# Another rate of gathers in each stage of a gMLP, SSD and PEER block

## The chip, the core and the metric

The kernel runs on one core of a Trainium2 chip. The metric is device time in microseconds (us) of one execution, as the median of several runs. Lower is better.

## The reference

One transformer block over 1024 tokens of width 1024, in float32. Cut to what matters here:

```python
h = x @ w_in                       # -> uv, z, xbc, dt_raw, gate_pre
ya = gmlp_branch(uv, ...) @ gm_w_out
yb = ssd_branch(z, xbc, dt_raw, ...) @ ssd_w_out
merged = gates[0] * ya + gates[1] * yb
x1 = layer_norm(ALPHA * x + merged @ w_o)
q = x1 @ w_q                       # 8 heads, two halves, 128 keys each
...                                # top 16 of each half, top 16 of their sums: 128 experts a token
act = gelu(einsum('tkd,td->tk', u_tab[experts], x1))
ch = einsum('tk,tkd->td', softmax_gates * act, v_tab[experts])
ple = sigmoid(x1 @ ple_w_gate + b) * (p @ ple_w_proj)
out = layer_norm(ALPHA * x1 + ch + ple)
```

`u_tab` and `v_tab` have 16384 rows of 1024 floats each, so each token needs 128 rows of either table.

## The kernel before

**Groups and stages.** The 1024 tokens are worked through in three groups of 2, 3 and 3 blocks of 128 tokens (`GROUPS`, here groups 0, 1 and 2). `front(gi)` (L218) runs one group through its stages: gMLP, SSD, merge, query (the product with `w_o`, the normalization, the products with `w_q`, the top 16, the PLE gate). Every matrix product is made of three fp32r passes (`mm3`, L155 to L157), and every weight tile is read by SyncE's DMA queue (`raw`), cast on ScalarE (`whi`, L149) and its rest taken on VectorE (`wlo`, L150).

**Two ways to apply the experts.** For groups 0 and 1 the rows that each token needs are gathered (`gather`, L835): one indirect DMA on GpSimd's queue brings 128 rows of 4 KB, one for each token of a block, into one of `RING` = 12 buffers named `row`. A U row is multiplied with the token and summed on VectorE (L856). Four V rows at a time go through products on TensorE (`pacc`, L898). A block takes 128 U and 128 V gathers, five blocks 1280 in all. For group 2 nothing is gathered: its stage "gates" (`dense_gates`, with `dense_scores` beside it) writes the gates of all 16384 experts to DRAM, and its stage "dense" (L988) multiplies the tokens with both whole tables, in 16 steps of 8 tiles of experts. The scores of 48 of the 128 tiles are computed ahead and kept in DRAM (`s`); the step that comes before one of these blocks of tiles reads them back (`ew<-s`, L1014), the others compute them.

**Side by side.** The gathers of group 0 are written into the program beside the stages of group 1, those of group 1 beside the rest of it and beside group 2. Their order within a gather group is: 70 U rows, then U and V rows in turn, and at the end 64 V rows alone. The order is written out by hand: `front` is a generator that yields a cost after each piece of work; the loop at the end of `block_kernel` (L1064 to L1074) adds the cost times the stage's rate to what is owed, and writes gathers, at 1.47 each, until nothing is owed. Which rate counts is `SIDE[phase[0]]` (L46):

```python
for cost in front(gi):
    owed += cost * SIDE[phase[0]]
    if not gate_t:
        owed = 0.0
    while side and owed > 0:
        step = next(side[0], None)
        ...
        owed -= step
```

The costs are in units of `UNIT` × blocks / 4, which is 4.01 for three blocks. A group of three blocks yields 33.6 units in the gMLP stage (8 for `w_v`, 9.6 for `w_u`, 16 for gates and output); in group 1 the last 24.4 of them come after the first gates exist. The SSD stage yields 66.2, the merge 16, the query stage 36.6 in a gather group and 58.6 in the dense group (with 22 score tiles), the gates 219.5 in plain cost, the dense stage 208 units and 14.4. What is left when `front(2)` has ended is written after it. `phase[0]` is 0 in the gMLP stage, 1 from the SSD stage to the end of the merge, 2 in the query stage, 3 in the gates and 4 in the dense stage.

**Other order.** A planner orders the instructions of each engine after the order written, with weights moved ahead by fixed offsets. A U row's multiply stands at least 6 gathers (`LAG`) behind its gather, and the products of four V rows at least 4 (`QLAG`). When the last gather block has 16 gathers left, two further ring buffers are filled with `ln2_g` and `ln2_b` (`finish_loads`, L793) for its normalization (`finish`, L799); the last dense step does the same for its own.

Of the kernel before, what the change touches and what calls it, by code (L numbers as in the profile page):

```python
# [42 lines left out]
AHEAD_G = 40  # L43
LEAD = 50
UNIT = 5.35
SIDE = (0.82, 0.78, 0.80, 0.66, 0.78)  # L46
ALPHA = 2 ** 0.25
EPS = 1e-5

# [32 lines left out]
def block_kernel(ctx, tc, a, out):  # L82
# [114 lines left out]
    ps, ps_es, phase, tk_, selects = {}, [None], [0], [None], []  # L197
# [20 lines left out]
    def front(gi):  # L218
# [310 lines left out]
            V.reciprocal(rrow, rrow)  # L529


        mp_es = ExitStack()
        mp = mp_es.enter_context(tc.tile_pool(name="mp", bufs=1, side=other))
        mh = mp.tile([128, 8, T], F32R, name="mh")
# [528 lines left out]
    for gi in range(NG):  # L1063
# [7 lines that stand above are left out]
                if step is None:  # L1071
                    side.pop(0)
                else:
                    owed -= step  # L1074
        if GROUPS[gi][1] == "gather":
            selects += [select(gi, c) for c in range(GROUPS[gi][0])]
            side += [experts([(gi, c, r0 + c * 128) for c in range(GROUPS[gi][0])])]
        r0 += GROUPS[gi][0] * 128
# [79 lines left out]
```

## Time and profile before

| | |
|---|---|
| median of 3 runs | 3757.99 us (3755.95 to 3758.19) |
| profiled execution, its own time | 3754.28 us |
| its span, first to last instruction | 3752.6 us |
| busy share of the span | TensorE 92%, VectorE 78%, ScalarE 47%, GpSimd 42% |
| granted TensorE clock, mean | 0.962 |
| moved by DMA | 1183.88 MB, 315 GB/s on average |

The stages in the span, read from the first and last instruction of their tiles (us from its start):

| stage | group 0 | group 1 | group 2 |
|---|---|---|---|
| gMLP | 0 to 112 | 520 to 713 (gathers from 563) | 1345 to 1548 |
| SSD | 112 to 340 | 713 to 1060 | 1548 to 1905 |
| merge | 340 to 400 | 1060 to 1137 | 1905 to 2002 |
| query | 400 to 520 | 1137 to 1345 | 2002 to 2310 |
| gates | | | 2310 to 2625 |
| dense | | | 2625 to 3673 |
| rest | | | 3673 to 3752.6 |

In the profile PE is TensorE's products, PEld its weight loads, DVE VectorE, ACT ScalarE, POOL GpSimd, SP SyncE. A busy share says how full an engine was in a stretch; PEclk is the granted share of TensorE's full clock, and the DMA share is the mean of the core's 16 DMA engines.

### The profile page before, as it was taken

How to read it: one execution, taken by the hardware profiler on the slowest of the kernel's cores; microseconds unless marked ns; L12 is line 12 of the kernel's file. 1: busy time of each engine (PE TensorE's matmuls, PEld its weight loads, DVE VectorE, ACT ScalarE, POOL GpSimd, SP SyncE). 2: the span in 40 equal slices, each digit the busy share in tenths (PEclk: the TensorE clock that was granted, in tenths of full speed). 3: DMA queues.
4: the chain of work that ended last, by engine and by line, in shares of the span. 5: the costliest groups of instructions: out<-in, count | busy, mean ns of one | idle time of the engine just before them, and what ended most of it. 6: DMA issues, size and time to landing. Idle time of an engine off the chain costs nothing. (4 is left out here: it accounts for less than half of the span.)

```text
span 3752.6 us, 59429 instructions
## 1 busy us (share of the span) xinstructions
PE 3439.9 (92%) x21390; PEld 2939.4 (78%) x21390; DVE 2935.7 (78%) x6823; ACT 1754.2 (47%) x2671; POOL 1569.2 (42%) x1310
## 2 busy tenths in 40 slices
PE   9899996999998988999987989889989999999995
PEld 8888896888887977888777878777768878778771
DVE  6677898898987989894698999997676676676652
ACT  6888443475752333475742334675333323233220
POOL 0000004744455444543455455334455455455544
PEclk9999998999999999999999999999999999999997
DMA  6444647989899787989899899899999999999987
GB/s 212 160 164 160 229 174 249 389 308 356 311 369 391 288 305 285 358 308 323 295 326 337 302 337 371 329 335 370 349 378 379 363 360 370 357 365 395 367 313 283
DMA packets 405703, 1183.88 MB, mean 315 GB/s; under 512 B 40736, under 2 KB 135968, under 8 KB 402336
## 3 DMA queue, kind: packets, MB, share of 16 engines
q0 software_dynamic: 187488, 682.71, 48.5%
q1 hardware_dynamic: 217200, 494.76, 36.8%
q8 instruction: 168, 2.75, 0.3%
q10 hardware_dynamic: 720, 2.62, 0.2%
q14 instruction: 127, 1.04, 0.1%
HBM read 1121.01 MB, written 58.92 MB: 314 GB/s over the span
## 5 line engine op out<-in xcount | busy, mean ns | idle before, releaser
L149 ACT CAST whi<-raw 128x1024 fp32r<-128x1024 f32 (+1 forms) x676 | 700.5, 1041 | 1127.2 <-PE mm L156 582.2
L837 POOL DMA_INDIRECT row<-in_peer_u_dram,idx x640 | 796.3, 1244 | 1004.3 <-PE pacc L898 376.2
L157 PE MATMUL mm<-xh,wlo 128*128 128x384 f32 (+2 forms) x3160 | 1055.3, 335 | 57.4 <-DVE wlo L150 50.5
L150 DVE TENSOR_TENSOR wlo<-raw,whi 128x1024 fp32r<-128x1024 f32 (+1 forms) x676 | 817.1, 1211 | 371.0 <-ACT whi L149 298.7
L155 PE MATMUL mm<-xh,whi 128*128 128x384 f32 (+2 forms) x3160 | 1060.6, 336 | 38.0 <-ACT whi L149 27.2
L156 PE MATMUL mm<-xl,whi 128*128 128x384 f32 (+2 forms) x3160 | 1046.8, 331 | 0.6 <-DVE xl L139 0.6
L837 POOL DMA_INDIRECT row<-in_peer_v_dram,idxT x640 | 758.9, 1186 | 681.9 <-DVE row L856 210.9
L856 DVE SCALAR_TENSOR_TENSOR row<-row,x1b 128x1024 f32<-128x1024 f32 x640 | 773.6, 1217 | 22.9 <-DMA row<-in_peer_u_dram,idx 18.5
L155 PEld LDWEIGHTS mm<-xh,whi 128*128 128x128 f32 (+1 forms) x3160 | 606.9, 192 | 93.4 <-ACT whi L149 51.5
L157 PEld LDWEIGHTS mm<-xh,wlo 128*128 128x128 f32 (+1 forms) x3160 | 606.1, 192 | 78.1 <-DVE wlo L150 60.1
L156 PEld LDWEIGHTS mm<-xl,whi 128*128 128x128 f32 (+1 forms) x3160 | 606.3, 192 | 9.5 <-issue 2.8
L898 PE MATMUL pacc<-row,zw 128*32 128x512 f32 x2560 | 321.3, 621 | 39.2 <-DMA row<-in_peer_v_dram,idxT 39.1
L155 PE MATMUL po<-whi,ewh 128*128 128x512 f32 x768 | 313.9, 409 | 20.1 <-DVE eacc L1051 17.9
L156 PE MATMUL po<-wlo,ewh 128*128 128x512 f32 x768 | 309.4, 403 | 17.1 <-DVE wlo L150 17.0
L157 PE MATMUL po<-whi,ewl 128*128 128x512 f32 x768 | 308.2, 401 | 0.0
L898 PEld LDWEIGHTS pacc<-row,zw 128*32 128x32 f32 x2560 | 68.5, 111 | 193.9 <-issue 140.6
L155 PEld LDWEIGHTS po<-whi,ewh 128*128 128x128 f32 x768 | 147.3, 192 | 86.3 <-DVE eacc L1051 19.9
L156 PEld LDWEIGHTS po<-wlo,ewh 128*128 128x128 f32 x768 | 147.5, 192 | 50.4 <-DVE wlo L150 18.5
L852 POOL DMA_DIRECT2D x1b<-x x5 | 3.0, 606 | 434.2 <-DMA x<-x 434.1
L138 ACT CAST ewh<-ew 128x384 fp32r<-128x384 f32 x128 | 65.6, 513 | 242.4 <-DVE ew L1019 175.3
L157 PEld LDWEIGHTS po<-whi,ewl 128*128 128x128 f32 x768 | 147.4, 192 | 36.1
L981 PE MATMUL mt<-o,o 128*128 128x128 f32 x768 | 148.9, 302 | 15.1 <-DVE o L979 6.0
(275 smaller groups left out, 5609.3 us busy)
## 6 DMA issues: line engine op xcount, KB each, us to landing
raw<-in_peer_uT_dram SPq DMA_DIRECT2D x128, 512.0 KB
raw<-in_peer_vd_dram SPq DMA_DIRECT2D x128, 512.0 KB
raw<-in_w_xbc_dram SPq DMA_DIRECT2D x96, 512.0 KB
raw<-in_w_g_dram SPq DMA_DIRECT2D x48, 512.0 KB
raw<-in_w_z_dram SPq DMA_DIRECT2D x48, 512.0 KB
raw<-in_ssd_w_out_dram SPq DMA_DIRECT2D x48, 512.0 KB
raw<-in_w_q_dram SPq DMA_DIRECT2D x48, 512.0 KB
g<-gt SPq DMA_DIRECT2D x24, 1024.0 KB
```

The source lines that it names most:

```text
L138: A.copy(hi, src)
L149: A.copy(hi, raw)
L150: V.tensor_sub(lo, raw, hi.bitcast(F32))
L155: PE.matmul(p, lhsT=lh, rhs=rh, start=start, stop=False, skip_group_check=skip)
L156: PE.matmul(p, lhsT=lh, rhs=rl, start=False, stop=False, skip_group_check=skip)
L157: PE.matmul(p, lhsT=ll, rhs=rh, start=False, stop=stop, skip_group_check=skip)
L837: g = POOL.indirect_dma_start(out=t, out_offset=None, in_=a[tab], in_offset=bass.IndirectOffsetOnAxis(ap=ix, axis=0))
L852: POOL.dma_start(x1, x1_d[gi, c])
L856: u = V.scalar_tensor_tensor(t, t, 1.0, x1, op0=OP.mult, op1=OP.mult, accum_out=act[:, k:k + 1])
L898: return PE.matmul(pacc[q * 32:q * 32 + 32, h * 512:h * 512 + 512], lhsT=zws[z][:, q, r % 4, :], rhs=ts[q][:, h * 512:h * 512 + 512], star ...
L981: PE.matmul(p[:, i, :], lhsT=o1, rhs=o2, start=True, stop=True)
```

## The change

`SIDE` gets new rates and a sixth entry, and the merge gets a phase of its own. The gMLP stage goes from 0.82 to 0.70, SSD from 0.78 to 0.82, the query stage from 0.80 to 0.68, the dense stage from 0.78 to 0.86, and the merge from the 0.78 of the SSD stage to 1.1. The gates keep 0.66.

```diff
-SIDE = (0.82, 0.78, 0.80, 0.66, 0.78)
+SIDE = (0.70, 0.82, 0.68, 0.66, 0.86, 1.1)
...
             V.reciprocal(rrow, rrow)


+        phase[0] = 5
         mp_es = ExitStack()
         mp = mp_es.enter_context(tc.tile_pool(name="mp", bufs=1, side=other))
```

## Rows read from the trace of the kernel before

**Rows 1.** The page: TensorE's busy time, and GpSimd's DMA queue (packets, MB, share).

```profile
PE 3439.9 (92%) x21390; PEld 2939.4 (78%) x21390; DVE 2935.7 (78%) x6823; ACT 1754.2 (47%) x2671; POOL 1569.2 (42%) x1310
...
q0 software_dynamic: 187488, 682.71, 48.5%
```

**Rows 2.** Windows by stage: length, PE, PEld, DVE, ACT, POOL, clock, DMA share, GB/s.

```profile
563.00:713.00 150.00, 120.25 (x640) 114.69 (x641) 140.34 (x315) 51.41 (x68) 90.59 (x65) 0.90 0.83 307
713.00:1060.00 347.00, 335.55 (x2199) 296.87 (x2198) 306.47 (x610) 239.74 (x386) 169.91 (x140) 0.99 0.89 331
1060.00:1137.00 77.00, 72.76 (x442) 64.54 (x441) 65.58 (x108) 27.48 (x35) 43.98 (x36) 0.98 0.98 374
1137.00:1195.00 58.00, 52.55 (x424) 44.49 (x423) 46.60 (x81) 20.11 (x32) 32.45 (x28) 0.98 1.02 395
1195.00:1297.00 102.00, 96.25 (x590) 84.98 (x591) 92.03 (x415) 31.52 (x49) 43.48 (x36) 0.96 0.84 316
...
1345.00:1460.00 115.00, 97.07 (x620) 80.95 (x620) 103.77 (x348) 51.89 (x73) 56.87 (x45) 0.92 0.84 309
...
1905.00:2002.00 97.00, 79.61 (x430) 74.49 (x428) 94.88 (x157) 34.11 (x48) 53.98 (x43) 0.93 0.95 346
...
2075.00:2165.00 90.00, 88.53 (x553) 78.35 (x552) 89.75 (x413) 30.46 (x48) 37.51 (x34) 1.00 0.85 302
2165.00:2310.00 145.00, 131.97 (x840) 117.56 (x839) 137.78 (x453) 55.03 (x64) 74.89 (x61) 0.96 0.94 355
...
2625.00:3673.00 1048.00, 1005.72 (x5131) 794.35 (x5133) 693.61 (x1067) 319.63 (x427) 529.60 (x447) 0.98 0.97 362
3673.00:3752.60 79.60, 34.76 (x193) 6.47 (x192) 15.25 (x29) 5.63 (x7) 38.83 (x40) 0.68 0.77 291
```

**Rows 3.** Windows view of the gathers alone (L837): POOL busy and count, then as above.

```profile
1060.00:1137.00 77.00, 43.98 (x36) 0.98 0.98 374
...
2625.00:3673.00 1048.00, 524.42 (x438) 0.98 0.97 362
3673.00:3752.60 79.60, 37.68 (x38) 0.68 0.77 291
```

**Rows 4.** Windows view of dense steps, all engines: two long, short, long, last.

```profile
2832.40:2907.60 75.20, 75.20 (x401) 61.85 (x400) 52.01 (x77) 23.10 (x30) 45.91 (x36) 1.00 0.99 379
2907.60:2984.90 77.30, 77.30 (x418) 62.17 (x416) 50.64 (x75) 25.43 (x34) 34.09 (x33) 1.00 0.97 358
2984.90:3033.00 48.10, 42.07 (x181) 30.35 (x178) 32.22 (x52) 11.68 (x17) 22.55 (x20) 0.89 0.99 357
...
3355.30:3430.60 75.30, 75.30 (x401) 61.85 (x400) 55.14 (x84) 25.54 (x32) 46.03 (x39) 1.00 1.03 403
...
3632.90:3673.00 40.10, 40.10 (x200) 28.10 (x200) 14.39 (x23) 7.34 (x8) 15.56 (x16) 1.00 0.74 260
```

**Rows 5.** Waits (total, times, longest), in dense and in 622 to 712.

```profile
DVE ew L1019 <- DMA ew<-s: 66.0, 16, 10.2
...
PEld mm L157 <- DVE wlo L150: 16.7, 3, 14.5
```

**Rows 6.** The chain that ended last, its end: start, us, what.

```profile
3731.78 6.26 DMA row<-in_peer_v_dram,idxT
3738.09 2.98 PE pacc L898 x16
...
3747.16 1.22 DVE x1b L808
```

**Rows 7.** Groups of instructions: the U multiply and its sum's read (count, busy, mean ns).

```profile
L856 DVE SCALAR_TENSOR_TENSOR row<-row,x1b 128x1024 f32<-128x1024 f32 x640 | 773.6, 1217 | 22.9 <-DMA row<-in_peer_u_dram,idx 18.5 <-issue 3.4
...
L856 DVE DVE_READ_ACCUMULATOR row<-row,x1b 128x1 f32 x640 | 51.7, 81 | 0.0
```

**Rows 8.** Windows view of the U multiplies alone (L856): DVE busy and count, then as above.

```profile
563.00:713.00 150.00, 68.46 (x115) 0.90 0.83 307
...
1905.00:2002.00 97.00, 50.36 (x84) 0.93 0.95 346
```

## The prediction

> **What bounds the kernel now.** I first read the page. TensorE is busy 92% of the span and GpSimd's DMA queue alone takes 48.5% of the 16 DMA engines [rows 1]. An average over unlike stages decides nothing, so I cut the span into stages with the windows view [rows 2]. In group 1's and group 2's gMLP and query stages VectorE is the fullest engine: 0.94 of 563:713, 0.90 of 1345:1460, 0.90 of 1195:1297, 1.00 of 2075:2165, 0.95 of 2165:2310, while the DMA share there is 0.83 to 0.94. The SSD stage (713:1060) has TensorE at 0.97 and DMA at 0.89. Merge and dense have DMA at 0.95 to 0.98. So the change takes gathers out of stages that are full on VectorE and puts them where DMA is full.
>
> A view of gathers per stage says whether the hand-made pacing is what the chip runs. The code gives a stage its cost × rate / 1.47 gathers. The merge of group 1 costs 16 units of 4.01 = 64.2, × 0.78 / 1.47 = 34, and the trace has 36; dense costs 208 units of 4.01 + 14 = 849, so 450, and the trace has 438; the last stretch gets the rest of 1280, 42, and the trace has 38 [rows 3]. The order written is the order run, within a ring buffer's run-ahead.
>
> Then the dense steps one by one [rows 4]. A step has 144 products with the expert table. In long steps (nine of sixteen) eight score tiles are computed as well, and TensorE is busy all of it: 75.2 us with 401 TensorE instructions, 77.3 with 418. The difference, one more group of 16 for four V rows, is 2.1 us. Short steps (five) take scores back from DRAM: 48.1 us, TensorE at 0.93 of full clock or under, DMA at 0.99. The last step does the same products in 40.1. In the view of waits, the multiply by the gates waits 66.0 us for these scores [rows 5]. Short steps are DMA-bound; long ones are bound by TensorE with DMA just below its limit. Last, the chain that ended last: after the products end at 3673, 38 gathers, a last landing (6.26 us), the product (2.98) and a normalization fill 79.6 us [rows 2, 3, 6].
>
> **Prices of a gather.** DMA: the queue's 48.5% of 3752.6 us over 1302 transfers of 512 KB (1280 gathers and 22 plain loads) is 1.40 us each [rows 1]. VectorE: a U row costs 1217 + 81 ns = 1.30 us [rows 7], a V row almost nothing; where they alternate, 0.65. TensorE: a V row costs 2.1 / 4 = 0.52 [rows 4], on average 0.26.
>
> **The change, part by part.** By the same formula:
> - gMLP, 0.82 to 0.70: group 1 has 24.4 units left once gates exist, so 55 to 47 gathers; group 2, 33.6 units, 75 to 64.
> - SSD, 0.78 to 0.82: 66 units, 141 to 148 in each group.
> - merge, 0.78 to 1.1: 34 to 48 in each.
> - query, 0.80 to 0.68: group 1, 36.6 units, 80 to 68; group 2, 58.6 units, 128 to 109.
> - gates, unchanged: 98.
> - dense, 0.78 to 0.86: 450 to 497.
> - rest, after everything: 42 to 4.
>
> No instruction is added or removed, and no wait is written in; all costs come from where the rows stand in in-order queues.
>
> *Rest.* 38 gathers were issued in the 59 us from 3673 to 3731.8 [rows 3, 6]. With 4 left, what remains is the dense blocks' own normalization and one landing, product and finish, as in the chain from 3731.78 on (about 21 us), plus a few gathers: some 30 us instead of 79.6. Gain 50; bounds 45 (a few more left over) and 59 (none).
>
> *Dense, +46.* Five short steps get 2 more each; they are DMA-bound, so 2 × 1.40 each, +14. Nine long steps get 3.6 more each. By TensorE that is 3.6 × 0.26 = 0.9 us a step; by DMA 5.0, less the about 2% (1.6 us) that DMA was free. One step moved 403 GB/s at a share of 1.03 and took no longer than the others [rows 4], so part of it still fits: I take 2 a step, +18. The other steps: +3. Sum +35; bounds 46 × 0.26 = 12 and 46 × 1.40 = 65. Here also the last gather block's two ln2 loads now fall into the last dense step, where the dense group holds two of the ring's 12 buffers as well; eight are left for the gathers. The last step's DMA share is 0.74 [rows 4], which covers this; without that cover it is a landing, 6 us, inside the bound.
>
> *Merge, +14 in each.* In group 1 DMA is full from 1060 to 1195 (0.98, 1.02) [rows 2]: 14 × 1.40 = 20, less what was taken from the query products right behind (3 gathers, 4 us) and what the next stage, at 0.84, can take over through prefetch: +10, bounds 4 (TensorE) and 20. In group 2 the merge lies in the stretch where group 1's U rows come alone: 50.4 us of U work in 97, VectorE at 0.98 [rows 2, 8]. The rows now land before the merge's own multiplies and weight splits in VectorE's queue, and TensorE waits for these: 14 × 1.30 = 18, less 3 in the stage behind, +15; bounds 9 and 20. Together +25.
>
> The merge's DMA row in group 1 is 0.98 at 374 GB/s, though half the requests come from GpSimd and half from SyncE. The Trainium skill (DMA: Bandwidth & Descriptors, section Issuing engines are not separate DMA queues) says that transfers of all issuing engines end on the same 16 DMA engines and interleave. By that rule every added gather delays weights, in merge and dense alike: the slower rival below. The sum above does not use it.
>
> *SSD, +7 in each.* TensorE: 7 × 0.26 = 2 each. Group 1 also gets U rows that left the gMLP stage (8 × 1.30) on a VectorE at 0.88: hidden behind TensorE, 1 more. +5; bounds 0 and 15.
>
> *gMLP, −8 and −11.* Group 1's are all U rows: 8 × 1.30 = 10 us less VectorE in a stage where it is 0.94 full. But the longest wait of TensorE there is one of 14.5 us for one weight split [rows 5], which a burst of VectorE work causes and a lower rate does not remove: −6. Group 2: 11 × 0.65 = 7, so −6. Together −12; bounds 0 and −18.
>
> *Query, −12 and −19.* × 0.65: 8 and 12 us of VectorE; TensorE is busy all but 2% of 2075:2165 [rows 2], so there only part is given back: −7 and −11; bounds 0 and −30, the latter at DMA price where its share is over 0.94.
>
> **Sum:** −50 + 35 + 25 + 5 − 12 − 18 = −15 us, from the profiled 3754.3 to 3739. The median is 3.7 above the profiled execution, so 3743.
>
> **Rivals.**
> 1. *DMA is the price everywhere (slower).* Dense pays 65 and merge 40: −50 + 65 + 40 + 5 − 12 − 18 = +30, 3788. For it: shares of 0.97 and 0.98 [rows 2]. Against it: TensorE without a gap in all long steps [rows 4]. It decides once a gather in dense costs over about 1.1 us (50 / 46), the merge as above.
> 2. *DMA has room (much faster).* Dense pays TensorE's price, 12, merge 4 + 15 (VectorE stays full there): −50 + 12 + 19 + 5 − 30 = −44, 3714. For it: the step at 403 GB/s. Against it: short steps wait for DMA. The Trainium skill (Perfetto Trace Analysis, section Identifying the Most-Contended Engine) says that occupancy of the DMA engines misleads and HBM use should be read instead. By that rule dense, at 362 GB/s on average [rows 2], still has 403 − 362 = 41 GB/s, a tenth, and this rival would hold; the short steps at 357 and waiting speak against it here.
> 3. *The relieved stages do not get shorter,* since bursts (top-16, selection) and not the gathers make VectorE late: −50 + 35 + 25 + 5 = +15, 3773. For it: the 14.5 us wait. Against it: U work alone is 68 of 150 us there.
> 4. *The pacing is not followed:* no change, 3758. Against it: [rows 3].
>
> **How the numbers follow.** What a measurement of this kernel can tell from no change is about 0.2%, 7.5 us. My forecast, with its own range of −38 to +5: 0.49; rival 1: 0.18; rival 2: 0.15; rival 3: 0.15; rival 4: 0.03. Faster: 0.15 and four fifths of mine, 0.54. Within 0.2%: a fifth of mine, a third of rival 3, rival 4: 0.18. Slower: rival 1 and the rest of rival 3: 0.28. The range goes from rival 2 (−44, a little more if the query stages return the full price) to rival 1 (+30): 3706 to 3788.
>
> **What would show it.** Right: some 4 gathers after the last dense product and a stretch there of about 30 us; long dense steps of 77 to 79 us and short ones of 50 to 51; both merges at 85 to 115 us; gMLP stages each some 6 us shorter. Wrong: long steps over 80 us or merges 20 us longer (rival 1), long steps at 76 (rival 2), gMLP and query lengths unchanged (rival 3). The prediction fails most easily in the price of a gather in a long dense step, which decides 30 of its us.

## The result and the profile after

The changed kernel takes 3731.78 us (median of 5 runs, 3727.95 to 3742.35) against 3757.99 us: ratio 0.9936, interval 0.9919 to 0.9952, so 0.6% faster. Its profiled execution took 3731.47 us with a span of 3729.8. On a second chip, where the kernel before had a median of 3772.24, the ratio was 0.993 (0.991 to 0.9949).

The first fence has the windows view of the changed kernel by stage, with the columns of [rows 2]; the borders are moved with the stages.

```profile
564.00:709.00 145.00, 119.73 (x632) 115.00 (x632) 135.00 (x305) 50.73 (x67) 81.93 (x59) 0.91 0.82 303
709.00:1064.00 355.00, 341.01 (x2241) 297.57 (x2241) 312.69 (x622) 237.89 (x384) 182.50 (x146) 0.99 0.90 328
1064.00:1150.00 86.00, 75.69 (x435) 64.54 (x434) 70.78 (x120) 26.68 (x35) 54.01 (x45) 0.94 1.02 398
...
1909.00:2024.00 115.00, 85.61 (x439) 79.73 (x436) 112.16 (x186) 34.12 (x48) 77.20 (x59) 0.87 0.98 365
...
2084.00:2174.00 90.00, 88.65 (x554) 80.08 (x553) 87.62 (x400) 29.93 (x48) 39.05 (x33) 1.00 0.78 288
2174.00:2309.00 135.00, 125.31 (x794) 112.41 (x794) 131.00 (x444) 52.04 (x62) 60.22 (x49) 0.97 0.93 339
...
2622.00:3709.30 1087.30, 1034.78 (x5321) 801.74 (x5319) 700.47 (x1079) 318.78 (x427) 562.46 (x495) 0.97 0.99 370
3709.30:3729.80 20.50, 3.82 (x33) 0.81 (x32) 14.21 (x25) 5.62 (x7) 0.56 (x1) 0.75 0.44 171
```

Against [rows 2], dense is some 39 us longer with DMA at 0.99, the stretch behind it fell from 79.6 to 20.5 us, and group 2's merge (1909:2024) has VectorE at 0.98 and TensorE at 0.74. The same view for the gathers alone, as in [rows 3]:

```profile
2622.00:3709.30 1087.30, 556.16 (x484) 0.97 0.99 370
3709.30:3729.80 20.50, 0.56 (x1) 0.75 0.44 171
```

One gather is issued behind dense instead of 38. The chain that ended last shows what is left there (columns as in [rows 6]): dense's own last sum and normalization (`eacc`) and then the gather block's (`x1b`), on VectorE with ScalarE between, and no row's landing any more.

```profile
3709.39 0.68 DVE eacc L1052
...
3714.64 2.35 DVE eacc L1058 x2
3717.06 1.12 DVE x1b L803
...
3724.73 1.23 DVE x1b L809
```

The dense steps, as in [rows 4]: the first, a long one, two short ones, the last long one and the last.

```profile
2661.30:2706.60 45.30, 41.97 (x194) 29.20 (x194) 30.85 (x49) 12.98 (x18) 19.94 (x17) 0.96 1.04 375
...
2837.30:2914.60 77.30, 77.30 (x418) 62.25 (x417) 53.59 (x81) 23.09 (x30) 41.94 (x38) 1.00 1.01 392
...
2991.80:3042.80 51.00, 41.45 (x182) 29.37 (x179) 33.14 (x60) 11.73 (x17) 19.78 (x21) 0.90 0.99 362
3317.50:3372.10 54.60, 41.22 (x181) 29.80 (x178) 36.07 (x58) 11.26 (x16) 28.45 (x26) 0.84 1.04 383
...
3579.70:3667.20 87.50, 87.50 (x498) 63.85 (x496) 33.21 (x46) 24.52 (x32) 35.03 (x37) 1.00 0.88 322
3667.20:3709.30 42.10, 42.10 (x216) 28.41 (x212) 13.79 (x19) 7.33 (x8) 19.39 (x21) 1.00 0.78 272
```

TensorE still has no gap in a long step, though DMA is now at 1.01 there; 77.3 instead of 75.2 us is one more group of four V rows. The last long step is 87.5 us, all of it TensorE: V rows that used to run behind dense are now in it. Before, this step and the first were:

```profile
2664.10:2701.90 37.80, 37.80 (x178) 27.78 (x177) 29.46 (x49) 13.26 (x18) 20.05 (x17) 1.00 1.03 374
...
3553.50:3632.90 79.40, 79.40 (x435) 62.63 (x433) 45.91 (x71) 24.79 (x33) 41.34 (x35) 1.00 0.90 342
```

The first step also reads eight scores back, so six steps are short, not five.

### The profile page after: what moved, and what is told of

It is laid out like the page before. It is cut to its first block, busy times and chain, and to the rows that moved or that the text cites. A ratio compares the mean times of both kernels' runs of the same rounds, so it can differ in the third digit from the quotient of the medians.

```text
span 3729.8 us, 59409 instructions
## 1 busy us (share of the span) xinstructions
PE 3437.4 (92%) x21390; PEld 2944.0 (79%) x21390; DVE 2934.5 (79%) x6823; ACT 1744.7 (47%) x2666; POOL 1551.4 (42%) x1310
## 5 line engine op out<-in xcount | busy, mean ns | idle before, releaser
L838 POOL DMA_INDIRECT row<-in_peer_u_dram,idx x640 | 786.8, 1229 | 937.6 <-PE pacc L899 299.3
L157 PE MATMUL mm<-xh,wlo 128*128 128x384 f32 (+2 forms) x3160 | 1054.9, 334 | 42.7 <-DVE wlo L150 41.0
L838 POOL DMA_INDIRECT row<-in_peer_v_dram,idxT x640 | 750.7, 1173 | 746.0 <-DVE row L857 245.0
L899 PE MATMUL pacc<-row,zw 128*32 128x512 f32 x2560 | 312.0, 605 | 15.1 <-DMA row<-in_peer_v_dram,idxT 15.1
L899 PEld LDWEIGHTS pacc<-row,zw 128*32 128x32 f32 x2560 | 67.2, 109 | 155.7 <-issue 131.5
L155 PE MATMUL mm<-whi,xh 128*128 128x256 f32 x512 | 148.4, 290 | 11.9 <-ACT whi L149 10.4
```

Source lines behind the costliest of these rows:

```text
L155: PE.matmul(p, lhsT=lh, rhs=rh, start=start, stop=False, skip_group_check=skip)
L157: PE.matmul(p, lhsT=ll, rhs=rh, start=False, stop=stop, skip_group_check=skip)
L838: g = POOL.indirect_dma_start(out=t, out_offset=None, in_=a[tab], in_offset=bass.IndirectOffsetOnAxis(ap=ix, axis=0))
L899: return PE.matmul(pacc[q * 32:q * 32 + 32, h * 512:h * 512 + 512], lhsT=zws[z][:, q, r % 4, :], rhs=ts[q][:, h * 512:h * 512 + 512], star ...
```

## The stages of all runs

A stage is counted here from its first instruction of one fixed kind (such as the merge's first sigmoid) to that of the next stage, so that runs can be compared; "relief" means the lower rates of the gMLP and query stages. Lengths in us, one profiled execution each. The first two columns are from one chip; the others were run where the kernel before had medians of 3772 to 3773 us, the last two beside the third and fourth.

| stage | before | after | before, 2nd | after, 2nd | dense only | merge only | relief only | more in SSD | merge back | dense 0.90 |
|---|---|---|---|---|---|---|---|---|---|---|
| gMLP 1 | 153.4 | 148.2 | 158.3 | 148.1 | 154.6 | 155.7 | 148.8 | 148.3 | 147.9 | 149.1 |
| SSD 1 | 348.3 | 356.7 | 352.3 | 362.3 | 350.6 | 352.2 | 348.3 | 370.4 | 358.1 | 357.5 |
| merge 1 | 83.1 | 92.1 | 82.6 | 91.3 | 83.7 | 92.3 | 82.7 | 90.9 | 84.1 | 84.9 |
| query 1 | 191.3 | 185.7 | 196.3 | 182.2 | 196.9 | 199.1 | 178.3 | 184.9 | 183.4 | 180.9 |
| gMLP 2 | 212.6 | 208.5 | 212.6 | 210.5 | 211.7 | 212.6 | 208.8 | 201.9 | 210.2 | 207.8 |
| SSD 2 | 372.7 | 373.5 | 375.3 | 372.8 | 378.5 | 389.4 | 357.9 | 406.1 | 362.6 | 362.0 |
| merge 2 | 89.2 | 107.2 | 87.0 | 107.8 | 89.9 | 106.1 | 94.0 | 98.9 | 94.5 | 96.6 |
| query 2 | 320.5 | 297.3 | 323.5 | 298.1 | 323.0 | 302.3 | 323.3 | 299.4 | 317.8 | 315.7 |
| gates | 329.3 | 327.4 | 338.5 | 333.6 | 334.3 | 329.7 | 339.3 | 335.6 | 336.7 | 333.4 |
| dense | 1008.9 | 1048.1 | 1008.9 | 1054.9 | 1048.5 | 1031.0 | 1016.5 | 1044.3 | 1040.7 | 1073.7 |
| rest | 79.6 | 20.4 | 80.5 | 20.4 | 19.4 | 42.3 | 147.4 | 19.9 | 58.3 | 30.4 |
| ratio to before, same chip | | 0.9936 | | 0.9930 | 0.9945 | 1.0024 | 1.0114 | 0.9976 | 0.9955 | 0.9971 |

## The experiments

Theory A is that of the prediction: a gather costs in each stage what the engine that is full there asks for it. Its rivals: only what is left at the end counts (B); the relief of the stages full on VectorE is the gain (C).

**One part at a time.** All of these are the changed kernel with other rates. Dense alone:

```diff
-SIDE = (0.70, 0.82, 0.68, 0.66, 0.86, 1.1)
+SIDE = (0.82, 0.78, 0.80, 0.66, 0.86, 0.78)
```

> The rates of before everywhere, only dense at 0.86: 42 gathers move from the stretch after the dense products into dense, none is left. Theory A (each stage has its own price, set by the engine that is full there): dense pays 0.85 us a gather as in the changed kernel, 36 us longer, the stretch at the end 59 us shorter, in all 20 to 25 us faster than before, within 5 us of the whole change. Theory B (only what is left at the end counts, a gather costs the same in every other stage): 20 to 25 us faster as well. Theory C (the relief of the stages full on VectorE is the gain): no gain, within 7 us of before.

Ratio 0.9945 (0.9928 to 0.9962), 21 us of 3773: A and B both give this, C falls. The dense stage is 1048.5 us and the rest 19.4, as in the whole change. So dense alone brings nearly all of the gain; what the other rates add, 3 to 6 us, is within the intervals.

The merge alone:

```diff
+SIDE = (0.82, 0.78, 0.80, 0.66, 0.78, 1.1)
```

> The rates of before everywhere, only the merge at 1.1: 14 more gathers in each merge, 14 instead of 42 left at the end. Theory A: group 1's merge 9 us longer, group 2's 18 us longer, of which the query stage behind gives some 10 back, the end 28 x 1.5 = 42 us shorter: 20 to 30 us faster. Theory B: 42 us less at the end and 28 x 0.85 = 24 more before it, 18 us faster, with both merges equally longer (12 us each). Theory C: slower or the same, since both merges are full and nothing is relieved.

Ratio 1.0024 (1.0008 to 1.004): 9 us slower, where A and B expected 18 to 30 us faster and only C "slower or the same". Against the first profile both merges are longer by what A said (9 and 17 us) and the rest is 37 us shorter. But two stages with unchanged rates are longer too, SSD 2 by 17 us and dense by 22. A had counted rows and not which rows: when more are taken early, group 1's lone U rows begin 14 places earlier, in SSD 2, and lone V rows of the end come into dense. The windows of the U multiplies in SSD 2 and of the V products in dense, in this run:

```profile
1577.40:1966.90 389.50, 59.36 (x98) 0.96 0.85 301
```

```profile
2704.90:3736.00 1031.10, 115.64 (x968) 25.14 (x968) 0.97 0.97 357
```

The same stretches of the kernel before:

```profile
1552.40:1925.10 372.70, 50.99 (x84) 0.99 0.87 313
```

```profile
2664.10:3673.00 1008.90, 109.72 (x916) 23.85 (x920) 0.98 0.97 364
```

8 us more U work in SSD 2, and three more groups of V products in dense, some 6 us of TensorE: that is half of SSD 2's 17 us and a quarter of dense's 22. Step by step, dense is 10 us longer in its first step, 7 in the other short ones and 5 in the long ones. So a gather's price depends on the kind of row that falls into a stage as well as on the stage; what the rest of the two sums is, this run does not settle.

The relief alone:

```diff
+SIDE = (0.70, 0.78, 0.68, 0.66, 0.78, 0.78)
```

> The rates of before everywhere, only the gMLP stage at 0.70 and the query stage at 0.68: 51 gathers more are left at the end (93). Theory A: gMLP stages 9 us shorter together, query stages 18 to 29 us shorter, the end 51 x 1.5 = 77 us longer: 39 to 50 us slower than before. Theory B: 51 x (1.5 - 0.85) = 33 us slower, each of the four stages shorter by 0.85 a gather. Theory C: the relieved stages shorter by over 40 us, at most 30 us slower.

Ratio 1.0114 (1.009 to 1.0138): 43 us slower, inside A's 39 to 50; B's 33 lies just outside the interval. The rest is 68 us longer instead of A's 77. The relief itself shows in gMLP 1, query 1 and gMLP 2 (5, 13 and 4 us); query 2 did not get shorter, because the lone U rows came later and fell into it: 79 rows are multiplied there, 72 before, though 20 fewer are gathered. SSD 2, which they left, is 15 us shorter at an unchanged rate, so A's total came out right with other parts than A's.

**More in SSD.**

```diff
+SIDE = (0.70, 0.94, 0.68, 0.66, 0.79, 1.1)
```

> As the changed kernel, but SSD at 0.94 and dense back at 0.79: 22 gathers more in each SSD stage (170), 41 fewer in dense, 1 left. Theory A: dense 41 x 0.85 = 35 us shorter than in the changed kernel; SSD, where TensorE is full and VectorE hides the U rows, pays TensorE's 0.3 to 0.5 us a gather, 13 to 22 us longer in all: 13 to 22 us faster than the changed kernel, 40 to 48 us faster than before. Theory B: the same as the changed kernel, within 7 us. A rival to A's price for SSD: DMA is at 0.89 there and 29 more gathers than before are 41 us of transfers in stages with 38 us free, so it fills up and pays 1.4 us for the last of them: no faster than the changed kernel.

Ratio 0.9976 (0.9962 to 0.9989), 15 us slower than the changed kernel's 0.9936 would be here, so A's price for SSD falls; but not to a full DMA. The windows view of this kernel's last part of SSD 2, all engines, and the same for the U multiplies alone, and then both for the changed kernel:

```profile
1860.00:1966.00 106.00, 83.36 (x481) 74.47 (x479) 101.15 (x183) 55.12 (x90) 52.14 (x40) 0.87 0.79 268
```

```profile
1860.00:1966.00 106.00, 48.48 (x81) 0.87 0.79 268
```

```profile
1829.00:1929.30 100.30, 90.70 (x622) 74.46 (x621) 78.65 (x140) 64.09 (x103) 48.09 (x42) 0.97 0.84 294
```

```profile
1829.00:1929.30 100.30, 14.40 (x24) 0.97 0.84 294
```

VectorE is at 0.95 with 48.5 us of U work, DMA at 0.79: the lone U rows lie in SSD 2 now and make it 33 us longer than in the changed kernel. SSD 1, where rows alternate, pays 14 us for 22 gathers (8 against the second profile).

A's price for dense falls here too. It expected dense 35 us shorter than in the changed kernel; with 37 fewer gathers in it, dense is 4 us shorter (11 against the second profile). Five groups of V products fewer would be some 10 us less, but one long step is 15 us longer than in the changed kernel:

```profile
2741.00:2833.70 92.70, 77.96 (x401) 63.65 (x400) 57.92 (x90) 26.36 (x34) 44.70 (x37) 0.91 0.95 353
```

TensorE is idle for 14.7 us of it, behind VectorE and a ScalarE that waits 16.6 us for a weight to land.

**The merge back, and then dense at 0.90.** Before these, both kernels once more on the same chip, unchanged.

> The kernel before, unchanged, to have its stages on the same chip as the next three. Each theory expects the stage lengths of the first profile, within the spread between chips.

> The changed kernel, unchanged, on the same chip as the next two. Theory A (each stage has its own price): 0.6 to 0.7% faster than before, merge 9 and 18 us longer, dense 39 us longer, the end 59 us shorter, long dense steps at 77.3 us (TensorE's price), short ones 2 to 3 us longer. If the stages differ by over 10 us from the first pair, the prices read from one pair of profiles are not prices of the stage.

Merges (8.7 and 20.8 us longer) and the rest (60 shorter) repeat within 3 us; dense is 46 us longer instead of 39, and the 7 lie in the six short steps (27 us longer instead of 21). This profile of the kernel before is from an execution of 3786.89 us, 15 above its median there; most of its other stages are 3 to 9 us longer than on the first chip, so a difference of that size in one stage of two profiles is weak evidence.

```diff
+SIDE = (0.70, 0.82, 0.68, 0.66, 0.86, 0.82)
```

> The changed kernel with the merge at 0.82 again: 12 gathers fewer in each merge, 28 instead of 4 left at the end. Theory A: the merges 12 x 0.64 = 8 and 12 x 1.3 = 16 us shorter, the query stage behind the second 5 to 10 us longer, the end 24 x 1.5 = 36 us longer: 17 to 22 us slower than the changed kernel. Theory M (the merge pays more than the end, as the run with the merge alone suggests, which was 9 us slower than before): 5 to 15 us faster than the changed kernel.

Ratio 0.9955 (0.9939 to 0.997), 11 us slower than the changed kernel's 3746.71 beside it: M falls, A's 17 to 22 was too much. The merges are 7 and 13 us shorter, SSD 2 10 and dense 14, query 2 is 20 us longer and the rest 38. So the merge at 1.1 earns its place, but only together with the other new rates; which of them it needs was not tried.

```diff
+SIDE = (0.70, 0.82, 0.68, 0.66, 0.90, 0.82)
```

> As the run before, with dense at 0.90: the 24 gathers that leave the merges go into dense (520 instead of 497), 5 left at the end. If dense charges TensorE's 0.26 us a gather (long steps at 77 to 79 us): dense 6 us longer, merges 24 us shorter: some 10 to 18 us faster than the changed kernel. If DMA, at a share of 1.01 in the long steps of the changed kernel, is at its edge there: 23 x 1.40 = 32 us longer, long steps over 80 us, so 5 to 10 us slower than the changed kernel.

Ratio 0.9971 (0.9955 to 0.9987), 17 us slower than the changed kernel, where the theory of a DMA at its edge said 5 to 10. Dense is 33 us longer than in the run before, for 23 gathers by the rates and 18 in the trace: 1.4 to 1.8 us each, DMA's price or more. The windows view of three of its steps, and two waits from 3376 to 3396 (total, times, longest):

```profile
2994.80:3050.00 55.20, 41.96 (x180) 30.12 (x177) 35.51 (x58) 11.77 (x18) 26.91 (x23) 0.85 0.99 366
3380.80:3470.40 89.60, 80.28 (x418) 63.63 (x417) 57.56 (x90) 25.65 (x34) 50.32 (x41) 0.94 1.01 383
3470.40:3547.70 77.30, 77.30 (x418) 62.24 (x416) 55.81 (x87) 24.00 (x32) 48.80 (x41) 1.00 1.03 399
```

```profile
DVE ew L1020 <- DMA ew<-s: 12.4, 2, 11.4
...
PE po L155 <- DVE eacc L1052: 9.3, 1, 9.3
```

Four of the five short steps are at 54 to 55 us. One long step with no more products than the others takes 89.6, with TensorE idle for 9 of them. It is no sign that long steps are now full: in it VectorE, which TensorE waits for, waits 11.4 us for the last score that the short step before it reads back, and that step took only 43.5. A short step's wait has moved over the border. The long step behind it ran at a share of 1.03 without a gap. With it, the six steps that read scores pay 29 of the 33 us.

**Which engine asks the price.** Two pairs, each of before and after with one cost halved. First the U multiply over half the width; the other half of each U row is left out of the sum.

```diff
-u = V.scalar_tensor_tensor(t, t, 1.0, x1, op0=OP.mult, op1=OP.mult, accum_out=act[:, k:k + 1])
+u = V.scalar_tensor_tensor(t[:, :512], t[:, :512], 1.0, x1[:, :512], op0=OP.mult, op1=OP.mult,
+                           accum_out=act[:, k:k + 1])
```

> The kernel before with the U multiply over half the width (VectorE 0.65 instead of 1.3 us a U row; the other half of each row is left out of the sum; transfers and TensorE unchanged). It is the base of the next run. Stages full on VectorE get shorter: gMLP of group 1 by 10 to 25 us, merge and query of group 2 by 10 to 25 us each; dense and the end as before, within 10 us.

> The changed kernel with the same half U multiply, to be held against the run before. Theory V (VectorE prices group 2's merge and the relief): merge of group 2 only 4 to 9 us longer instead of 18, query of group 2 5 to 13 us shorter instead of 23, gMLP of group 1 0 to 3 us shorter instead of 5; merge of group 1 still 7 to 11 longer, dense still 35 to 45 longer, the end still 59 shorter. Theory D (DMA prices all of these): group 2's merge still 16 to 20 us longer, the query stage still some 20 us shorter.

The multiply fell from 1217 to 686 ns. Medians 3707.12 and 3677.57. Group 2's merge is now 85.3 and 88.4 us; here it is in the before and the after of this pair:

```profile
1908.60:1993.90 85.30, 74.69 (x428) 73.32 (x429) 68.10 (x150) 25.11 (x34) 49.92 (x43) 0.92 1.02 398
```

```profile
1896.50:1984.90 88.40, 77.28 (x428) 73.93 (x429) 72.85 (x163) 28.17 (x37) 56.80 (x48) 0.90 1.02 397
```

3 us longer instead of 18, with DMA full in both: VectorE had asked some 15 of those 18, though here only 5 more rows are multiplied in this merge and 14 with whole multiplies. Query 2 is 14 us shorter instead of 23 and gMLP 1 2 instead of 5; merge 1 is 12 us longer, dense 36, the rest 58 shorter, none of which VectorE explains. Theory V holds, missing three of its ranges by 1 us, and D falls. Neither had named SSD 1 and SSD 2, which are 8 us shorter each here instead of 8 and 1 longer; the profile of the before is from an execution 9 us above its median. Of the base's own expectations, gMLP 1 and group 2's merge and query came out only 3 to 5 us shorter than in the first profile, not 10 to 25.

Then half rows in the gathers, 2 KB instead of 4; the half that comes is used twice, the other left out.

```diff
-g = POOL.indirect_dma_start(out=t, out_offset=None, in_=a[tab],
+g = POOL.indirect_dma_start(out=t[:, 512:], out_offset=None, in_=a[tab].rearrange("n (h d) -> (n h) d", h=2),
...
-u = V.scalar_tensor_tensor(t, t, 1.0, x1, op0=OP.mult, op1=OP.mult, accum_out=act[:, k:k + 1])
+u = V.scalar_tensor_tensor(t.rearrange("p (h n) -> p h n", h=2),
+                           t[:, 512:].unsqueeze(1).to_broadcast([128, 2, 512]), 1.0,
+                           x1.rearrange("p (h n) -> p h n", h=2), op0=OP.mult, op1=OP.mult,
+                           accum_out=act[:, k:k + 1])
...
-rhs=ts[q][:, h * 512:h * 512 + 512],
+rhs=ts[q][:, 512:],
```

> The kernel before with gathers of half a row (2 KB instead of 4 KB a partition; the half that comes is used twice, so the other half is left out; the work of VectorE and TensorE is unchanged). It is the base of the next run. If short dense steps wait for DMA, they fall from 48 us to 38 to 41, and dense is 40 to 60 us shorter; the end is limited by GpSimd's 1.25 us a gather, 60 to 75 us.

> The changed kernel with the same half rows, to be held against the run before. If DMA prices dense's short steps and the merge of group 1: dense 12 to 20 us longer instead of 39 (TensorE's price alone), merge of group 1 2 to 5 us longer instead of 9, merge of group 2 still 12 to 20 longer by VectorE. If dense pays something else than transfers (places in the ring, queues): still 35 to 45 us longer.

Medians 3668.33 and 3623.43: the change now gains 45 us instead of 26. In the before of this pair the five short steps fell from between 46 and 53 us to between 38 and 45, and dense by 43. Merge 1, merge 2 and dense, before and then after:

```profile
1073.70:1151.20 77.50, 75.71 (x466) 68.82 (x466) 62.56 (x101) 28.02 (x36) 43.78 (x34) 0.98 0.84 282
1906.80:1990.20 83.40, 71.03 (x413) 67.21 (x414) 82.83 (x133) 24.51 (x33) 47.54 (x38) 0.98 0.80 259
2622.70:3588.80 966.10, 960.82 (x4953) 756.33 (x4955) 673.29 (x1035) 305.25 (x406) 544.10 (x439) 1.00 0.80 262
```

```profile
1052.60:1133.40 80.80, 79.14 (x498) 68.24 (x499) 71.88 (x123) 27.88 (x35) 65.39 (x50) 1.00 0.90 306
1883.30:1989.40 106.10, 82.28 (x440) 78.34 (x441) 100.39 (x164) 27.04 (x35) 71.45 (x54) 0.89 0.78 246
2604.00:3589.30 985.30, 981.29 (x5129) 757.70 (x5130) 674.86 (x1043) 305.51 (x406) 585.43 (x484) 1.00 0.82 270
```

Dense is 19 us longer instead of 39, at TensorE's price, with TensorE at over 0.99; merge 1 is 3 us longer instead of 9; merge 2 stays 23 us longer (V's range here ended at 20) though DMA is at 0.78 there, which shows VectorE's price without a full DMA. The first dense step before and after, and one short step of the changed kernel, with half rows:

```profile
2622.70:2662.30 39.60, 38.12 (x178) 27.75 (x177) 30.62 (x49) 12.89 (x18) 19.62 (x17) 1.00 0.93 314
```

```profile
2604.00:2643.90 39.90, 39.90 (x194) 28.16 (x193) 31.34 (x51) 13.06 (x18) 20.56 (x16) 1.00 0.98 330
...
2916.40:2954.40 38.00, 38.00 (x181) 27.96 (x178) 33.66 (x57) 11.83 (x17) 23.95 (x21) 1.00 1.03 356
```

38.0 us at full clock, and 38 to 41 in all five, where whole rows take 45 to 55: the wait for the scores was a wait for bandwidth that the gathers take. This agrees with the rule of the Trainium skill (DMA: Bandwidth & Descriptors, section Issuing engines are not separate DMA queues) that the prediction weighed. Of the 21 us that the change costs in the six short steps with whole rows, none is left; the 19 us are in the long steps and the last.

None of the six other sets of rates beat the changed kernel.

## Why the prediction was right

Forecast 3743 and faster, measured 3731.8. Of the 11 us between them 8 are the terms below; the rest is the distance of the median from the profiled execution, 3.7 us in the kernel before and 0.3 in the changed one. The terms against the two profiles of the first chip:

| term | predicted | measured |
|---|---|---|
| rest | −50 | −59 |
| dense | +35 | +39 |
| both merges, less 3 behind | +25 | +27 |
| SSD | +5 | +9 |
| gMLP | −12 | −9 |
| query | −18 | −29 |
| span | −15 | −23 |

*Rest.* The place was right; I had left a few gathers behind dense, and there is one, so the upper bound came true.

*Dense.* That this term came so close is in part luck. The five short steps are 14 us longer, as said, and by DMA, as the half rows show; but they take 45 to 55 us, not 50 to 51, and on the second chip the 14 are 24. The long steps are 16 us longer instead of 18, but not by DMA as half of that sum supposed: TensorE's own price is higher than I had put it, and 8 of the 16 are in the last long step alone. The row counts show it, first before, then after, for the V products alone (PE, PEld, clock, DMA, GB/s):

```profile
2625.00:3673.00 1048.00, 111.64 (x932) 24.26 (x936) 0.98 0.97 362
```

```profile
2622.00:3709.30 1087.30, 132.77 (x1108) 28.82 (x1108) 0.97 0.99 370
```

176 more, 11 groups at 2.1 us, is 23 us (the half rows measure 19); my bound of 12 took half of the moved rows for U rows, and those that leave the end are all V rows: dense multiplies 44 more V rows and 2 more U rows. With 23, rival 2 would have given −33. The rest of dense's 39 lies in the short steps, and in the first step, 45.3 us instead of 37.8, the sixth that reads scores back, which I had not counted.

*Merges.* Group 1 by DMA and group 2 by VectorE, with 9 and 18 us, as the two pairs show separately. The 3 us that I took back behind the second merge were too few; they lie in the next point.

*Query.* The term that was most off: query 2 is 23 us shorter instead of 11 to 14. Lone U rows that the merge takes early no longer fall into the products with `w_o` behind it. That this, and not only the lower rate, is the cause is shown by the run with the merge alone, where the rate of the query stage is unchanged and it is 18 us shorter. The windows of the U multiplies in query 2 (two records a row), in the kernel before, the changed kernel and the run with the merge alone:

```profile
2014.30:2334.80 320.50, 87.27 (x144) 0.96 0.90 328
```

```profile
2036.50:2333.90 297.40, 69.10 (x114) 0.98 0.87 317
```

```profile
2072.90:2375.20 302.30, 73.06 (x120) 0.98 0.94 349
```

That is 72, 57 and 60 rows. With the merge back at 0.82 it is 70 rows and 317.8 us. In query 1, I had taken VectorE for the fullest engine of 1195:1297; by [rows 2] TensorE is, with 96 of 102 us against 92.

*Rivals.* Rival 1 (DMA's price everywhere) does not hold at 0.86. At 0.90 dense paid as much as that price, 33 us, but mostly in the steps that read scores back, not everywhere. Rival 2 holds for the long steps. The Trainium skill's rule beside it (Perfetto Trace Analysis, section Identifying the Most-Contended Engine) agrees with the long steps, which ran at a DMA share of 1.01 without a gap, and not with the short ones. Rival 3 fails, as gMLP and query 1 were shorter in every run with their lower rates. Rival 4 fails by the counts.

What stays open is why SSD 1 pays 8 to 10 us for 7 gathers: with half the U multiply it is 8 us shorter and with half rows 5 longer, which points to VectorE, but it was not tried alone. The first dense step's 7.5 us go with the bytes: with half rows it takes 39.6 and 39.9 us. And no single price of a gather describes dense over all runs: 1031.0 us with the merge alone and 1044.3 with more in SSD, at 433 and 437 gathers, stand beside 1008.9 at 432.

## What to carry to other kernels

Price a movable piece of work stage by stage, by the engine that is full there, and count which kind of piece falls where: one rate changed early shifts every later piece, so a part measured alone (the merge, 9 us slower) can have the other sign within the whole (11 us faster). When work can run beside a stage that ends with idle engines, empty that end first; here it is most of the gain. Before a rate is raised further, look at the steps that wait already: the next pieces are paid there first, while the average still shows room.

## What the runs showed of the hardware

A DMA share of 1.00 is no sharp limit. Long dense steps ran at 1.01 to 1.03 and 382 to 399 GB/s with TensorE never idle, and a short one lost 13 us at 0.99 and 362 GB/s, where scores come in beside the gathers. With half rows a short step ran at 1.03 and 356 GB/s and lost nothing. Short steps also paid twice for waiting: the granted clock, 1.00 in a step without a gap, was 0.84 to 0.96 in those of the changed kernel, so part of each stretch ran at 1.2 GHz. Of the 13 us, TensorE was idle for 9.5, and its products took 3.5 longer (41.45 us busy against 38.00).
